# Multi-query attention on one core: the next batch's query loads and DMA transposes dealt out over the whole batch

## The chip, the cores and the metric

The kernel runs on one core of a Trainium2 chip. The metric is the device time of one execution in microseconds (us). Three runs of the kernel before gave 773.25, 774.67 and 776.23 us; the median is 774.67 us.

## The reference

Softmax attention with 16 query heads that share one key head and one value head. There are 8 batches of 1024 positions, and a head has 64 elements. All tensors are float32.

```
scores = np.matmul(q, k.transpose(0, 1, 3, 2)) / np.sqrt(head_dim)
weights = np.exp(scores - np.max(scores, axis=-1, keepdims=True))
weights = weights / np.sum(weights, axis=-1, keepdims=True)
attn_out = np.matmul(weights, v)
```

## The kernel before, in words

**Steps.** The work is cut into 1024 steps, 128 for each batch: eight pairs of heads, for each pair two chunks of 512 queries, for each chunk eight blocks of 128 keys. `step(u)` makes the scores of one block for two heads: two TensorE matmuls (L249) fill one PSUM tile `sc` of 128 x 1024 float32. There are three `sc` buffers. Four of five steps take the exponential on ScalarE (ACTIVATE, L262, 824 of them). Each fifth step takes it on VectorE by arithmetic on the bits (`vector_exp`: L213 reads the PSUM tile and frees it; L219, L229, L237 and L239 follow, SBUF to SBUF). The program recorded which buffer each `sc` tile gets: after a VectorE step the buffer comes back three steps later, and in some places four.

**Values.** The product with V runs some 18 steps behind the scores, as many small matmuls (L323) into PSUM tiles `ot` of seven groups, of which there are two. When a tile is full, VectorE inverts the sums (L265) and scales the result (L274), and SyncE stores it (L302). After the last group of a batch VectorE also tests the range of the sums (function `check`: L369, L375 and L379 over 128 columns); this falls at steps 21 to 27 of the next batch.

**The order of the work.** The order is written out by hand: each engine and each DMA queue takes its instructions in the order in which Python emits them, and waits on semaphores. `plan()` deals the value matmuls over the steps, and `after(u)`, called behind step u, emits the preparation of the next batch b+1:

- `load_kv` (L99, on SyncE): K of the next batch into `knat`.
- `load_v` (L106, on GpSimd): V into one of two constant tiles `vp`; it must wait until TensorE has used the V that lies there, which is that of batch b-1.
- `load_q` (L123, on GpSimd): 128 rows of queries, cast to fp16, into one of eight `q16` buffers. Eight of these in a batch.
- `turn_q` (L133, on SyncE): a DMA transpose of one such buffer into the tile `qt`, of which there are two. Eight in a batch.
- `prep_k` (L192, on GpSimd): two TENSOR_SCALAR that scale K into fp16, followed on SyncE by one DMA transpose (L196) into `k2t`.
- `prep_v` (L204, on VectorE): two small TENSOR_SCALAR that scale V.

Before, these stand at steps 48 (K and V), 48 to 62 (a query load in every second step), 64 to 78 (a transpose in every second step), 84 (`prep_k`) and 88 (`prep_v`) of the batch. The scores of the next batch read the first half of `qt` from step 128 and the second half from step 136 (counted from the start of batch b).

GpSimd's queue has nothing else in it. So GpSimd does not run at the steps at which its work is emitted: it runs ahead until an instruction has to wait. SyncE's queue also has the 129 stores, each of which waits for its L274; this holds SyncE near the step at which its work was emitted.

Of the kernel before, what the change touches and what calls it, by code (L numbers as in the profile page):

```python
# [30 lines left out]
def attention_main(ctx, tc, q, k, v, out, flag):  # L31
# [14 lines left out]
    NKT = S // P  # L46
# [46 lines left out]
    def load_kv(b):  # L93
        st = kv.setdefault(b, {})
        st["knat"] = kvp.tile([P, NKT, D], FP32, tag="knat", name=f"knat{b}")
        n = 2 if b == 0 else 1
        for h in range(n):
            js = slice(h * NKT // n, (h + 1) * NKT // n)
            nc.sync.dma_start(  # L99
                out=st["knat"][:, js, :],  # L100
                in_=k[b].rearrange("(c p) d -> p c d", p=P)[:, js, :],
            )
        st["vp"] = vps[b % 2]

    def load_v(b):
        nc.gpsimd.dma_start(  # L106
            out=vps[b % 2][:, 0, :, 0:D], in_=v[b].rearrange("(c p) d -> p c d", p=P)
        )
# [10 lines left out]
    def load_q(b, c):  # L119
        h0 = 2 * NFIRST if b == 0 else 0  # L120
        t = q16p.tile([P, H * D], FP16, tag="q16", name=f"q16_{b}_{c}")
        q16[(b, c)] = t[:, h0 * D :]
        nc.gpsimd.dma_start(  # L123
            out=q16[(b, c)],
            in_=q[b, c * P : (c + 1) * P, h0:, :].rearrange("p h d -> p (h d)"),
        )

    def turn_q(b, c):

        p0 = NFIRST if b == 0 else 0  # L130
        if b not in qt:
            qt[b] = qtp.tile([P, HP, S], FP16, tag="qt", name=f"qt{b}")
        nc.sync.dma_start_transpose(  # L133
            out=qt[b][:, p0:, c * P : (c + 1) * P], in_=q16.pop((b, c))
        )

    def bank(name):
        return op.tile([P, 512], FP32, tag="ot", name=name)
# [32 lines left out]
    def first_q(ps, p, cs):  # L171
        for c in cs:
            nc.tensor.matmul(  # L173
                ps[:, c * P : (c + 1) * P],
                q16[("first", p)][:, c, :],
                ident16,
                is_transpose=True,
                start=True,
                stop=True,
            )  # L180

    def first_q_out(ps, p, cs, eng):
        if 0 not in qt:
            qt[0] = qtp.tile([P, HP, S], FP16, tag="qt", name="qt0")
        at = slice(cs[0] * P, (cs[-1] + 1) * P)
        eng(out=qt[0][:, p, at], in_=ps[:, at])  # L186

    def prep_k(b):
        st = kv[b]
        k16d = kvp.tile([P, NKT, 2, D], FP16, tag="k16d", name=f"k16d_{b}")  # L190
        for i in range(2):
            nc.gpsimd.tensor_scalar(  # L192
                out=k16d[:, :, i, :], in0=st["knat"], scalar1=kscale, scalar2=None, op0=ALU.mult
            )
        st["k2t"] = kvp.tile([P, S], FP16, tag="k2t", name=f"k2t{b}")
        nc.sync.dma_start_transpose(  # L196
            out=st["k2t"].rearrange("p (j s) -> p j s", j=NKT),
            in_=k16d.rearrange("p j i d -> p (j i d)"),
        )

    def prep_v(b):
        vp = kv[b]["vp"]
        for i, ci in ((1, C0), (2, C3)):
            nc.vector.tensor_scalar(  # L204
                out=vp[:, i, :, 0:D], in0=vp[:, 0, :, 0:D], scalar1=ci, scalar2=None, op0=ALU.mult
            )
# [176 lines left out]
    PSTEPS = NCH * NKT  # L383
# [38 lines left out]
    def after(u):  # L422
        p, r = divmod(u, PSTEPS)
        b, hp = divmod(p, HP)
        if u == 1:
            first_q(turned[0], 0, range(NKT // 2, NKT))
            first_q_out(turned[0], 0, range(NKT // 2, NKT), nc.vector.tensor_copy)
        if r == 7 and p + 1 < NFIRST:
            turned[p + 1] = bank(f"qps{p + 1}").bitcast(FP16)
            first_q(turned[p + 1], p + 1, range(NKT))  # L430
            first_q_out(turned[p + 1], p + 1, range(NKT), nc.vector.tensor_copy)
        if b + 1 < B:
            at = hp * PSTEPS + r - 3 * PSTEPS
            if at == 0:
                load_kv(b + 1)
                load_v(b + 1)
            if 0 <= at < 2 * NKT and at % 2 == 0:
                load_q(b + 1, at // 2)
            at -= PSTEPS
            if 0 <= at < 2 * NKT and at % 2 == 0:  # L440
                turn_q(b + 1, at // 2)
            at -= PSTEPS
            if at == 4:
                prep_k(b + 1)
            if at == 8:
                prep_v(b + 1)

    with tc.manual_schedule():
        load_kv(0)
# [31 lines left out]
        for u in range(STEPS):  # L481
# [27 lines left out]
            for x in us:  # L509
                after(x)  # L510
# [97 lines left out]
@with_exitstack  # L608
def kernel(ctx, tc, q, k, v, out):
    nc = tc.nc  # L610
    fp = ctx.enter_context(tc.tile_pool(name="flagp", bufs=1))
    flag = fp.tile([1, 1], I32, name="flag")
    attention_main(tc, q, k, v, out, flag)
    bad = nc.values_load(flag, min_val=0, max_val=1)
    with tc.If(bad != 0):
        attention_general(tc, q, k, v, out)
# [30 lines left out]
```

## Time and profile before

| what | value |
|---|---|
| median of three runs | 774.67 us (773.25 to 776.23) |
| the profiled execution | 773.22 us |
| its span, first to last instruction | 771.4 us |
| granted TensorE clock, mean | 0.998 |
| GpSimd busy | 66.9 us (9%) |
| DMA engines: share of queue 1 (SyncE's) and queue 0 (GpSimd's) | 32.7% and 15.2% |
| mean rate of all DMA | 96 GB/s |
| stores of 256 KB, issue to landing, median | 2.5 us |
| query loads of 256 KB, issue to landing, median | 8.7 us |

A group's row in the page gives its line, engine and operation, what it writes and reads, the count, the busy time, the mean duration in ns, and the idle time of the engine just before it with what ended it. ScalarE's instructions overlap: one ACTIVATE is recorded with 1085 ns, but the next starts about 904 ns behind it (the median of the 823 intervals between their starts in the trace). [...] "SPq" is SyncE's queue.

### The profile page before, as it was taken

The page shows a single profiled execution, that of the slowest core. Times are in us where ns is not written, and L with a number is a line of the kernel's source. Part 1 is how long each engine was busy: PE and PEld are TensorE (multiplying, and loading weights), DVE is VectorE, ACT ScalarE, POOL GpSimd, SP SyncE. Part 2 cuts the span into 40 slices and gives each one's busy share as a digit, 9 for nine tenths or more (in the row PEclk, how much of TensorE's full clock was granted, in tenths as well). Part 3 has the DMA queues.
Part 4 walks back from the last instruction along what each step waited for, and adds up shares of the span by engine and source line. Part 5 has one row for each costly group of instructions (what it writes and reads, how often), then busy time and mean ns, then how long its engine had stood idle before and what let it go on. Part 6 is the DMA issues. An engine that isn't in the chain of part 4 may idle for free.

```text
span 771.4 us, 30670 instructions
## 1 busy us (share of the span) xinstructions
PE 744.1 (96%) x13474; PEld 471.9 (61%) x13474; DVE 730.3 (95%) x1349; ACT 759.3 (98%) x827; POOL 66.9 (9%) x99
## 2 busy tenths in 40 slices
PE   6999999999999999999999999999999999999997
PEld 2566666666666666666666666666666666666665
DVE  3899999999999999999999999999999999999993
ACT  7999999999999999999999999999999999999996
POOL 4110002100111002010020100200002100000000
PEclk9999999999999999999999999999999999999999
DMA  9949219471283814657246552566516474111112
GB/s 176 149 88 166 57 43 159 91 146 57 38 165 85 150 30 79 137 112 110 57 88 141 114 97 57 82 134 117 106 43 121 96 137 85 43 44 56 44 44 85
DMA packets 168633, 73.84 MB, mean 96 GB/s; under 512 B 93744, under 2 KB 161328, under 8 KB 168496
## 3 DMA queue, kind: packets, MB, share of 16 engines
q1 hardware_dynamic: 148864, 53.76, 32.7%
q0 software_dynamic: 18576, 17.57, 15.2%
q8 instruction: 106, 1.74, 1.0%
q10 hardware_dynamic: 1056, 0.52, 0.3%
q14 instruction: 31, 0.25, 0.1%
HBM read 37.75 MB, written 33.55 MB: 92 GB/s over the span
## 4 chain that ended last, share of the span: by engine, by line
PE 40%; ACT 35%; issue 12%; DVE 12%; DMA 1%; ACTq 0%; DVEq 0%
ACT wt L262 35%; PE ot L323 22%; PE sc L249 18%; DVE we L213 4%; DVE osb L274 2%; DVE we L239 2%; DVE mm L237 2%; DVE we L229 1%; DVE m L219 1%; DMA qf<-in_q_dram 1%; DVE rec_all L265 0%; PE otl L353 0%; DVE both L375 0%; DVE ok_all L379 0%; DVE ge L369 0%
## 5 line engine op out<-in xcount | busy, mean ns | idle before, releaser
L262 ACT ACTIVATE wt<-sc 128x1024 f16<-128x1024 f32 x824 | 756.8, 1085 | 2.0 <-PE sc L249 1.7
L323 PE MATMUL ot<-vp,wt 128*128 128x65 f16 x6528 | 430.1, 194 | 0.8 <-DVE osb L274 0.8
L323 PEld LDWEIGHTS <-wt 128*128 128x128 f16 x6528 | 328.2, 98 | 133.7 <-issue 133.5
L249 PE MATMUL sc<-qt,k2t 64*128 64x512 f16 x2048 | 364.6, 388 | 16.2 <-ACT wt L262 12.1
L323 PE MATMUL ot<-vp,we 128*128 128x65 f16 x4800 | 351.7, 193 | 0.0
L323 PEld LDWEIGHTS <-we 128*128 128x128 f16 x4800 | 251.6, 97 | 44.4 <-issue 44.4
L213 DVE TENSOR_SCALAR we<-sc 128x1024 int16<-128x1024 f32 x200 | 243.4, 1217 | 12.0 <-PE sc L249 11.1
L249 PEld LDWEIGHTS <-k2t 64*128 64x128 f16 x2048 | 86.3, 94 | 108.7 <-issue 75.7
L237 DVE TENSOR_TENSOR mm<-m 128x1024 f16<-128x1024 f16 x200 | 136.4, 682 | 0.0
L239 DVE TENSOR_TENSOR we<-we,mm 128x1024 f16<-128x1024 f16 x200 | 136.1, 681 | 0.0
L274 DVE TENSOR_TENSOR osb<-ot,rec_all 128x448 f32<-128x448 f32 x146 | 90.7, 621 | 5.1 <-DVE rec_all L265 0.2
L219 DVE TENSOR_SCALAR m<-we 128x1024 int16<-128x1024 int16 x200 | 85.8, 429 | 0.0
L229 DVE TENSOR_SCALAR we<-we 128x1024 int16<-128x1024 int16 x200 | 85.3, 426 | 0.0
L106 POOL DMA_DIRECT2D vp<-in_v_dram x8 | 7.8, 980 | 377.7 <-PE ot L323 377.6
L123 POOL DMA_DIRECT2D q<-in_q_dram x64 | 34.5, 570 | 26.3 <-DMA qt<-q 22.5
L265 DVE RECIPROCAL rec_all<-ot 128x7 f32<-128x7 f32 x146 | 28.5, 195 | 7.2 <-PE ot L323 7.2
L192 POOL TENSOR_SCALAR k16d<-knat 128x512 f16<-128x512 f32 x14 | 22.4, 1611 | 137.7 <-DMA knat<-in_k_dram 115.9
L157 PE MATMUL kps<-ident,k 128*64 128x128 f16 x16 | 1.3, 314 | 4.4 <-DVE k L148 4.4
L204 DVE TENSOR_SCALAR vp<-vp 128x512 f16<-128x512 f16 x16 | 3.9, 284 | 1.5 <-DMA vp<-in_v_dram 1.5
L186 DVE COPY qt<-qps 128x512 f16<-128x512 f16 (+1 forms) x2 | 1.1, 554 | 4.0 <-PE qps L173 4.0
L157 PEld LDWEIGHTS <-k 128*64 128x64 f16 x16 | 0.8, 159 | 4.6 <-DVE k L148 4.6
L466 ACT ACT_TABLE_LOAD x1 | 1.3, 1283 | 1.9 <-issue 1.9
(29 smaller groups left out, 22.4 us busy)
## 6 DMA issues: line engine op xcount, KB each, us to landing
out_dram<-osb SPq DMA_DIRECT2D x127, 256.0 KB, 2.5
q<-in_q_dram POOLq DMA_DIRECT2D x56, 256.0 KB, 8.7
knat<-in_k_dram SPq DMA_DIRECT2D x7, 256.0 KB, 3.7
q<-in_q_dram POOLq DMA_DIRECT2D x8, 192.0 KB, 7.4
vp<-in_v_dram POOLq DMA_DIRECT2D x8, 128.0 KB, 4.1
qt<-q SPq DMA_TRANSPOSE x64, 3.7
qf<-in_q_dram ACTq DMA_DIRECT2D x2, 256.0 KB, 4.3
knat<-in_k_dram SPq DMA_DIRECT2D x2, 128.0 KB, 3.6
```

The lines of the kernel that those rows point to most:

```text
L123: nc.gpsimd.dma_start(out=q16[(b, c)], in_=q[b, c * P : (c + 1) * P, h0:, :].rearrange("p h d -> p (h d)"),)
L192: nc.gpsimd.tensor_scalar(out=k16d[:, :, i, :], in0=st["knat"], scalar1=kscale, scalar2=None, op0=ALU.mult)
L213: nc.vector.tensor_scalar(out=t, in0=sc, scalar1=15.0 * 1024, scalar2=0.0, op0=ALU.add, op1=ALU.max)
L219: lambda: nc.vector.tensor_scalar(out=m.bitcast(I16), in0=t, scalar1=0x3FF, scalar2=0x3C00, op0=ALU.bitwise_and, op1=ALU.bitwise_or,)
L229: lambda: nc.vector.tensor_scalar(out=w3[:, 0].bitcast(I16), in0=t, scalar1=0x7C00, scalar2=None, op0=ALU.bitwise_and,)
L237: pend.append(lambda: nc.vector.tensor_tensor(out=m2, in0=m, in1=m, op=ALU.mult))
L239: lambda: nc.vector.tensor_tensor(out=w3[:, 2], in0=w3[:, 1], in1=m2, op=ALU.mult)
L249: nc.tensor.matmul(sc[:, hh, :], k2t[r : r + 64, j * P : (j + 1) * P], qt[b][r : r + 64, p % HP, c * QCH : (c + 1) * QCH], start=True, sto ...
L262: nc.scalar.activation(out=w, in_=sc, func=EXP, scale=escale, bias=math.log(CS))
L265: nc.vector.reciprocal(out=rec_all[:, g0 : g0 + n], in_=o[:, 0:n, D])
L274: nc.vector.tensor_tensor(out=ob[:, i0 : i0 + n, :], in0=o[:, 0:n, 0:D], in1=rec.unsqueeze(2).broadcast_to([P, n, D]), op=ALU.mult,)
L323: nc.tensor.matmul(o[:, gg % GB, 0 : D + 1], w[:, hh, qb * P : (qb + 1) * P], vp[:, i, j, 0 : D + 1], start=(n == 0), stop=last,)
```

## The change

Only the places in `after(u)` change, no instruction. K's load moves from step 48 to step 2, V's from 48 to 30, `prep_k` from 84 to 58 and `prep_v` from 88 to 72. The eight query loads move to steps 4, 17, 30, ... 95 and the eight transposes to steps 24, 37, 50, ... 115, both 13 steps apart.

```
         if b + 1 < B:
-            at = hp * PSTEPS + r - 3 * PSTEPS
-            if at == 0:
+            at = hp * PSTEPS + r
+            if at == 2:
                 load_kv(b + 1)
+            if at == 30:
                 load_v(b + 1)
-            if 0 <= at < 2 * NKT and at % 2 == 0:
-                load_q(b + 1, at // 2)
-            at -= PSTEPS
-            if 0 <= at < 2 * NKT and at % 2 == 0:
-                turn_q(b + 1, at // 2)
-            at -= PSTEPS
-            if at == 4:
+            if at == 58:
                 prep_k(b + 1)
-            if at == 8:
+            if at == 72:
                 prep_v(b + 1)
+            c, late_by = divmod(at - 4, 13)
+            if 0 <= c < NKT and late_by == 0:
+                load_q(b + 1, c)
+            c, late_by = divmod(at - 24, 13)
+            if 0 <= c < NKT and late_by == 0:
+                turn_q(b + 1, c)
```

The order of the built program shows what this does on each engine. TensorE's and ScalarE's instructions stand as before, and so do the reuse of the `sc` buffers and all waits between the compute engines. On VectorE `prep_v` stands some 20 instructions earlier in each batch. On SyncE the transposes stand one by one between the stores. On GpSimd the order within a batch was V, eight query loads, `prep_k`; it is now query loads 0 and 1, V, query loads 2, 3 and 4, `prep_k`, query loads 5, 6 and 7.

## Prediction
> **What bounds the kernel now.** I read the page's busy times first, then ScalarE's group, then the waits around the places where ScalarE loses time.
>
> ```profile
> PE 744.1 (96%) x13474; PEld 471.9 (61%) x13474; DVE 730.3 (95%) x1349; ACT 759.3 (98%) x827; POOL 66.9 (9%) x99
> ...
> L262 ACT ACTIVATE wt<-sc 128x1024 f16<-128x1024 f32 x824 | 756.8, 1085 | 2.0 <-PE sc L249 1.7
> ```
>
> ScalarE is idle for only 2.0 us ahead of its 824 ACTIVATEs. In the trace the first starts at 7.2 us and the last ends at 765.4 us, and most intervals between starts are 0.903 to 0.904 us. The floor of that stretch is 823 x 0.9033 + 1.1 = 744.5 us; it takes 758.1 us, so 13.6 us are above the floor. I added up this excess by sixteenths of a batch (columns of 16 steps, over all eight batches): steps 64 to 79, with nearly all query transposes, have 1.35 us; steps 96 to 111, which have no preparation at all, have 1.33 us. The columns of steps 16 to 31 and 32 to 47 have 3.11 and 2.20 us. So **the transposes cost ScalarE nothing today, and spreading them has nothing to win**. The excess behind step 16 has one other source:
>
> ```profile
> 497.92 0.22 DVE L369 TENSOR_SCALAR ge<-rec_all 128x128 f32<-128x128 f32 x1
> 498.17 0.29 DVE L375 SCALAR_TENSOR_TENSOR both<-rec_all,ge 128x128 f32<-128x128 f32 x1
> 498.50 0.29 DVE L379 TENSOR_REDUCE ok_all<-both 128x1 f32<-128x128 f32 x1
> 498.70 1.21 DVE L213 TENSOR_SCALAR we<-sc 128x1024 int16<-128x1024 f32 x1
> ```
> ```profile
> PE sc L249 <- DVE we L213: 0.4, 1, 0.4
> ACT wt L262 <- PE sc L249: 0.4, 1, 0.4
> ```
>
> This is VectorE's timeline in batch 5, and the waits of 495 to 501 us. The range test takes 0.78 us (497.92 to 498.70). L213 starts late by that much, the `sc` buffer comes back late, TensorE waits for it, and ScalarE for TensorE. VectorE cannot absorb it: a cycle of five steps lasts 3.00 us without a result tile (L213 at 498.70, the next at 501.70) and 3.77 us with one (314.69 to 318.46), and five of seven cycles have one: 3.55 us on average, against 4 x 0.903 = 3.61 us of ScalarE. That is **0.06 us of slack per five steps**. Taking 0.29 us as a batch's usual excess over steps 16 to 47, the range tests cost 0, 0.35, 0.52, 0, 0.60, 0.56 and 0.26 us in batches 1 to 7, together 2.3 us. (In batch 0 the 0.7 us at 20 to 24 us come ahead of the full TensorE clock; the edit does not touch them.)
>
> A stall begins where L213 starts more than some 0.92 us behind the preceding ACTIVATE if its buffer returns after three steps (L213's 1.17 us and the two matmuls with ScalarE's start, 0.62 us, against 3 x 0.903 us), or 1.82 us after four. Behind the range test that distance is 1.32, 1.69, 1.12, 1.37, 1.49 and 1.43 us in batches 1 to 6; in 1, 2, 4 and 6 the buffer at that place returns after four. So any VectorE delay that meets the range test is paid nearly in full by ScalarE, there or within 25 steps (the distance still reaches 0.98 at step 48 of batch 4).
>
> **What the change moves.** GpSimd is not where its steps say. V's load waits for TensorE, and all behind it follows at once:
>
> ```profile
> 115.25 0.95 POOL L106 DMA_DIRECT2D vp<-in_v_dram  x1 [62.08 <-PE ot L323]
> 116.20 4.29 POOL L123 DMA_DIRECT2D q<-in_q_dram  x8
> ```
> ```profile
> L192 POOL TENSOR_SCALAR k16d<-knat 128x512 f16<-128x512 f32 x14 | 22.4, 1611 | 137.7 <-DMA knat<-in_k_dram 115.9
> ```
>
> First GpSimd's timeline in batch 1, at step 16: V and eight query loads in one go, although emitted at steps 48 to 62. Below it the page's row of `prep_k`: its wait is for K, which SyncE loads at step 48, so it runs at steps 43 to 58, far from the range test.
>
> *Query loads.* They do not spread as written. Loads 0 and 1 now stand ahead of V, in the batch before, behind their `q16` buffers' transposes. Loads 2 to 7 still follow V's wait. No transposition needs them before step 50. Price nothing.
>
> *K and `prep_k`.* K is loaded at step 2 and lands some 3.7 us (5 steps) after its issue, ahead of step 16. So `prep_k` no longer waits for K: it follows V (0.95 us) and three query loads (3 x 0.53 us), 2.54 us behind V's start, for 2 x 1.48 us. That is steps 19 to 24, **just ahead of the range test**. What it does to VectorE is seen in batch 2 (timelines of VectorE and of GpSimd):
>
> ```profile
> 234.79 0.42 DVE L219 TENSOR_SCALAR m<-we 128x1024 int16<-128x1024 int16 x1
> 235.13 0.83 DVE L229 TENSOR_SCALAR we<-we 128x1024 int16<-128x1024 int16 x1
> ```
> ```profile
> 235.07 2.95 POOL L192 TENSOR_SCALAR k16d<-knat 128x512 f16<-128x512 f32 x2 [20.60 <-DMA knat<-in_k_dram]
> ```
>
> L229 starts 0.06 us into the GpSimd instruction and takes 0.83 instead of 0.42 us. Over the seven executions of `prep_k`, L219 and L229 together were lengthened by 0.41, 0.58, 0.41, 0.41, 0.41, 0.27 and 0.61 us; the other VectorE instructions were not. Putting the new place (V's start + 2.54 us) on the old timeline: in batches 1, 2, 4 and 5 an L219 starts inside it (117.82, 212.70, 400.93 and 495.71 us); in 3 and 6 none does, by 0.4 us and less. I take one hit of 0.41 us in each of the four (1.64), and half a hit in each of the two (0.41). The query loads that stand there now already lengthen L219 and L229 by 0.19, 0.04 and 0.17 us in batches 2, 4 and 5; this goes with the loads that are displaced: -0.40. `prep_k` in its old place costs ScalarE about 0.1 us (batch 6, steps 48 to 63, 0.27 against 0.19): -0.1. Both ends: no hit at all, -0.5; two hits in all six batches, 12 x 0.41 = +4.9. I take the rows' own places, nearer the lower end. Batch 0's `prep_k` comes at some 31 us, with no range test near: nothing.
>
> [...]
>
> *Transposes.* Same 64, dispatched in 1.3 us each on SyncE.
>
> ```profile
> qt<-q SPq DMA_TRANSPOSE x64, 3.7
> ```
>
> The last one is emitted at step 115 and needed when TensorE, some two steps ahead, scores step 136: 19 steps x 0.73 us = 14 us against 3.7 us to landing. The fourth stands at step 63 and is needed at 126. Stores that queue behind one transpose wait 1.3 us; an output buffer is reused a whole tile (seven stores, about 40 us) later, so nobody waits. If a transpose took the trace's maximum of 14.8 us (at the start, beside eight loads), that cover would be gone.
>
> *`prep_v`.* Two instructions of 0.28 us go from step 88 to 72. At 88 no excess is seen (1.45 us in that column against 1.33); at 72 the distance is 0.3 to 0.8 us and will be less without `prep_k` shortly before. V has landed long since. Price nothing.
>
> **Sum:** 1.64 + 0.41 - 0.40 - 0.1 = +1.5 us on the profiled 773.22 us (span 771.4 and 1.8 around it): 774.8. The median shown is 1.45 us above that execution, so I add the same to it: **776.2 us**, +0.2%. About 0.5% (3.9 us) is what a measurement here can tell from no change.
>
> **Rivals.**
>
> 1. *No hit counts* (0.20): the GpSimd instructions fall between L229 and the next L219, or the delay falls into VectorE's waits (0.04 us from TensorE's end before batch 3's step 21). -0.5 us: 774.2. For it: batches 3 and 6 do this on the old timeline. Against: all seven old executions hit.
> 2. *Clearly slower: the result banks* (0.16). A later VectorE also empties `ot` later, and TensorE with 96% busy has to wait for a bank, as in batch 6 (waits of 596 to 601 us):
>
> ```profile
> PE ot L323 <- DVE osb L274: 0.5, 1, 0.5
> ```
>
> It decides once L274 behind the range test ends later than TensorE's first matmul of the next-but-one tile, as there. Six full hits (2.5) and five more such waits of 0.5 us: +5.0, 779.7 us. Against: only 0.8 us of such waits in the whole span.
> [...]
> 4. *A late transpose* (0.02): at 14.8 us to landing, TensorE waits about 1 us at seven batch ends: +8.5 with the sum above, 783.
> 5. *Faster by over 0.5%* (0.02): all 2.3 us of range test stalls and more would have to go; no row shows how.
>
> My forecast has 0.56. Range 773.2 to 779.8 us: from rival 1 less 1 us of run-to-run spread to the upper bound of the hits, which takes in rival 2. Faster by over 0.5% 0.03, within 0.5% 0.77 (forecast, rival 1, most of rival 3), slower 0.20 (rivals 2, 4, and the forecast's upper tail).
>
> **What would show it.** In the profile after: L192 right behind three L123 at steps 19 to 24 with no wait for K in batches 1 to 6; L219 or L229 of 0.8 us there; more excess at steps 24 to 48 in batches 1, 2, 4, 5; transposes with no TensorE wait behind them. If L192 still runs at steps 43 to 58, or the excess behind the range test does not grow, I am wrong. If TensorE waits at steps 128 or 136, rival 4 holds.

## The result, and the profile after

The changed kernel takes 783.53 us (median of 6 runs, 782.05 to 786.79), the kernel before 773.97 us on the same chip (6 runs, 773.25 to 776.23): **slower by 1.2%, ratio 1.0123 (95% interval 1.0104 to 1.0141)**. The forecast was +0.2%, 776.2 us, with a range up to 779.8. The profiled execution of the changed kernel took 782.26 us, its span is 780.4 us and its mean granted clock 0.992.

First the page of the kernel after: busy times, three groups (busy, mean ns of one, idle time before them and what ended it) and one row of DMA issues. The last line here is L219's group in the kernel before.

```profile
PE 743.4 (95%) x13474; PEld 472.1 (60%) x13474; DVE 736.0 (94%) x1349; ACT 760.6 (97%) x827; POOL 67.4 (9%) x99
...
L262 ACT ACTIVATE wt<-sc 128x1024 f16<-128x1024 f32 x824 | 758.1, 1082 | 9.7 <-PE sc L249 9.0
...
L219 DVE TENSOR_SCALAR m<-we 128x1024 int16<-128x1024 int16 x200 | 89.0, 445 | 0.0
...
L192 POOL TENSOR_SCALAR k16d<-knat 128x512 f16<-128x512 f32 x14 | 22.9, 1648 | 12.3 <-DMA knat<-in_k_dram 12.3
...
qt<-q SPq DMA_TRANSPOSE x64, 4.0
```
```profile
L219 DVE TENSOR_SCALAR m<-we 128x1024 int16<-128x1024 int16 x200 | 85.8, 429 | 0.0
```

ScalarE now waits 9.7 us ahead of its ACTIVATEs, where it waited 2.0. VectorE is busy for 736.0 us instead of 730.3 with the same 1349 instructions, so some of them became longer: L219 from 429 to 445 ns on average. L192's wait for K fell from 115.9 to 12.3 us, all of it in batch 0. The transposes land 4.0 us after their issue (median; before 3.7).

The waits over the whole span (total us, times, longest) show the way on which the time reaches ScalarE, first after, then before:

```profile
ACT wt L262 <- PE sc L249: 9.0, 12, 1.5
PE sc L249 <- DVE we L213: 7.4, 8, 1.6
...
PE ot L323 <- DVE osb L274: 1.8, 4, 0.7
```
```profile
ACT wt L262 <- PE sc L249: 1.7, 4, 0.7
...
PE sc L249 <- DVE we L213: 1.0, 3, 0.4
...
PE ot L323 <- DVE osb L274: 0.8, 2, 0.5
```

TensorE waits 7.4 us for L213 (before: 1.0 us), and for a result bank it waits 1.8 us (before: 0.8). It has no wait for a transpose in this profile.

The excess over ScalarE's floor of 0.9033 us per ACTIVATE, added up as in the prediction, went from 13.58 to 22.53 us: +8.95, which is nearly the whole difference of the two profiled executions (782.26 - 773.22 = 9.04). By sixteenths of a batch it was 1.32, 3.11, 2.20, 1.46, 1.35, 1.45, 1.33, 1.36 us; it is 1.34, **10.19, 4.41**, 1.14, 1.37, 1.41, 1.34, 1.34. So all of the increase lies at steps 16 to 47, in batches 1 to 6. The columns in which the transposes used to stand alone (64 to 79) did not move.

GpSimd's and VectorE's timelines at that place in batch 1:

```profile
115.03 0.91 POOL L106 DMA_DIRECT2D vp<-in_v_dram  x1 [71.31 <-PE ot L323]
115.92 1.62 POOL L123 DMA_DIRECT2D q<-in_q_dram  x3
117.53 3.64 POOL L192 TENSOR_SCALAR k16d<-knat 128x512 f16<-128x512 f32 x2
```
```profile
117.01 0.75 DVE L239 TENSOR_TENSOR we<-we,mm 128x1024 f16<-128x1024 f16 x1
117.68 2.14 DVE L219 TENSOR_SCALAR m<-we 128x1024 int16<-128x1024 int16 x1
119.75 0.82 DVE L229 TENSOR_SCALAR we<-we 128x1024 int16<-128x1024 int16 x1
```

`prep_k` follows V and three query loads, 2.50 us behind V's start (forecast 2.54), at step 19. But the L219 that meets it takes 2.14 us instead of 0.42, and L229 0.82. The forecast had one lengthening of 0.41 us here. Batch 4, the same two engines:

```profile
406.60 3.65 POOL L192 TENSOR_SCALAR k16d<-knat 128x512 f16<-128x512 f32 x2
```
```profile
406.99 1.04 DVE L219 TENSOR_SCALAR m<-we 128x1024 int16<-128x1024 int16 x1
407.95 0.95 DVE L229 TENSOR_SCALAR we<-we 128x1024 int16<-128x1024 int16 x1
408.83 1.08 DVE L237 TENSOR_TENSOR mm<-m 128x1024 f16<-128x1024 f16 x1
```

Three VectorE instructions in a row are lengthened, by 0.62, 0.54 and 0.40 us (undisturbed they take 0.42, 0.42 and 0.68). L237 was never lengthened in the profile before. I call the sum over a batch, of what each VectorE instruction beside GpSimd takes above its undisturbed time, the **lengthening**. In batches 1 to 6 it is 2.20, 2.05, 0.42, 1.67, 0.96 and 1.35 us: 8.64 us in all, mean 1.44 (of the 8.64, L219 has 5.0, L229 1.9, L237 1.2 and L239 0.5). In the kernel before it was 0.44 to 0.74, mean 0.54.

And batch 2, where the delay meets the range test:

```profile
214.76 2.15 DVE L219 TENSOR_SCALAR m<-we 128x1024 int16<-128x1024 int16 x1
...
218.67 0.22 DVE L369 TENSOR_SCALAR ge<-rec_all 128x128 f32<-128x128 f32 x1
...
219.45 1.22 DVE L213 TENSOR_SCALAR we<-sc 128x1024 int16<-128x1024 f32 x1
```

L213 starts 3.54 us behind the preceding ACTIVATE; by the prediction's estimate the stall begins at 0.92 or 1.82. Behind the range test the largest distance before was 1.69 us.

### The profile page after: what moved, and what is told of

The parts are those of the page before. It is cut to its first block, busy times and chain, and to the rows that moved or that the text cites. A ratio compares the mean times of both kernels' runs of the same rounds, so it can differ in the third digit from the quotient of the medians.

```text
span 780.4 us, 30655 instructions
## 1 busy us (share of the span) xinstructions
PE 743.4 (95%) x13474; PEld 472.1 (60%) x13474; DVE 736.0 (94%) x1349; ACT 760.6 (97%) x827; POOL 67.4 (9%) x99
## 4 chain that ended last, share of the span: by engine, by line
PE 38%; ACT 34%; DVE 14%; issue 12%; DMA 1%; DVEq 0%; ACTq 0%
ACT wt L262 34%; PE ot L323 21%; PE sc L249 17%; DVE we L213 4%; DVE mm L237 2%; DVE osb L274 2%; DVE we L239 2%; DVE m L219 2%; DVE we L229 1%; DMA qf<-in_q_dram 1%; DVE rec_all L265 0%; DMA out_dram<-osb 0%; PE otl L353 0%; DVE both L375 0%; DVE ok_all L379 0%
## 5 line engine op out<-in xcount | busy, mean ns | idle before, releaser
L262 ACT ACTIVATE wt<-sc 128x1024 f16<-128x1024 f32 x824 | 758.1, 1082 | 9.7 <-PE sc L249 9.0
L213 DVE TENSOR_SCALAR we<-sc 128x1024 int16<-128x1024 f32 x200 | 243.5, 1217 | 15.9 <-PE sc L249 15.3
L237 DVE TENSOR_TENSOR mm<-m 128x1024 f16<-128x1024 f16 x200 | 137.7, 688 | 0.0
L239 DVE TENSOR_TENSOR we<-we,mm 128x1024 f16<-128x1024 f16 x200 | 136.8, 684 | 0.0
L219 DVE TENSOR_SCALAR m<-we 128x1024 int16<-128x1024 int16 x200 | 89.0, 445 | 0.0
L229 DVE TENSOR_SCALAR we<-we 128x1024 int16<-128x1024 int16 x200 | 85.6, 428 | 0.0
L192 POOL TENSOR_SCALAR k16d<-knat 128x512 f16<-128x512 f32 x14 | 22.9, 1648 | 12.3 <-DMA knat<-in_k_dram 12.3
```

Source lines behind the costliest of these rows:

```text
L192: nc.gpsimd.tensor_scalar(out=k16d[:, :, i, :], in0=st["knat"], scalar1=kscale, scalar2=None, op0=ALU.mult)
L213: nc.vector.tensor_scalar(out=t, in0=sc, scalar1=15.0 * 1024, scalar2=0.0, op0=ALU.add, op1=ALU.max)
L219: lambda: nc.vector.tensor_scalar(out=m.bitcast(I16), in0=t, scalar1=0x3FF, scalar2=0x3C00, op0=ALU.bitwise_and, op1=ALU.bitwise_or,)
L229: lambda: nc.vector.tensor_scalar(out=w3[:, 0].bitcast(I16), in0=t, scalar1=0x7C00, scalar2=None, op0=ALU.bitwise_and,)
L237: pend.append(lambda: nc.vector.tensor_tensor(out=m2, in0=m, in1=m, op=ALU.mult))
L239: lambda: nc.vector.tensor_tensor(out=w3[:, 2], in0=w3[:, 1], in1=m2, op=ALU.mult)
```

## The experiments

Each ratio is against the kernel before on the same chip, with its 95% interval. "Lengthening" is per batch, mean of batches 1 to 6, from the run's profile.

**1. Only K goes back** (`e1_k_late`). K's load returns to step 48; the rest of the change stays.

```
-            if at == 2:
+            if at == 48:
                 load_kv(b + 1)
```

> The changed kernel with one edit undone: K is loaded at step 48 again, so that prep_k waits for it and runs at steps 43 to 58 as before; query loads 5, 6 and 7 stay behind it. All transposes and loads stay spread. Theory A (the whole loss is prep_k running on GpSimd between the query loads, just ahead of the range test): the time falls back to that of the kernel before, 773 to 775 us, and the excess of steps 16 to 47 from 14.6 to about 5.3 us. Rival B (the spread transposes, stores behind them, or the two early query loads cost): it stays at 780 us or more. If 6 of the 9.6 us go, both have a part.

775.5 us (773.3 to 777.97), ratio 1.0020 (1.0003 to 1.0037), just above what was expected; lengthening 0.47. With K late, `prep_k` waits for it again and starts at steps 45 to 60. 7.8 of the 9.6 us are gone (+1.8 left), with all the transposes and loads in their new places. In the profile of this run the rest has a place of its own: steps 32 to 47 of batch 0, where TensorE waits for one of batch 0's query transposes.

```profile
PE sc L249 <- DMA qt<-q: 2.0, 1, 2.0
```

The first transpose of batch 1 now stands close behind those of batch 0, and took 9.1 us to dispatch. But experiment 10, whose transposes stand as in the kernel before, has the same wait with 0.9 us, so that the change causes it is not shown.

**2. Only `prep_k` moves** (`e2_k_early_alone`). The kernel before, with K's load at step 2 and `prep_k` behind the third query load; loads and transposes stay as they were.

```
+            if hp == 0 and r == 2:
+                load_kv(b + 1)
             if at == 0:
-                load_kv(b + 1)
                 load_v(b + 1)
...
+            if at == 4:
+                prep_k(b + 1)
```

> The kernel before with prep_k moved alone: K is loaded at step 2, and prep_k stands behind V and three query loads on GpSimd, as in the changed kernel; the transposes stay in their burst at steps 64 to 78. Theory A: 781 to 785 us, with L219 and L229 lengthened by some 1.4 us a batch at steps 19 to 24. Rival B: 774 to 776 us.

780.05 us (779.28 to 781.64), ratio 1.0082 (1.0057 to 1.0106), just under what was expected; lengthening 1.31. So the move of `prep_k` alone makes 0.8 of the 1.2%. In this profile the granted clock does not fall (0.998 on average) and TensorE has no wait for nothing that the profile shows; the changed kernel's profile has both (see the last section). What makes the other 0.4% was not separated; a repeat of the changed kernel (9) gave 0.9%.

**3. No `prep_k`** (`e11_no_prep_k`). The changed kernel; batches 2 to 7 take the keys of batch 1, without `prep_k` and its transpose, so their scores are of the wrong keys.

```
+        if b > 1:
+            st["k2t"] = kv[1]["k2t"]
+            return
```

> The changed kernel with prep_k left out for batches 2 to 7: they use the transposed K of batch 1, so the scores of these batches are of the wrong keys; K is still loaded. Loads, transposes and stores stay as in the changed kernel. Theory A: with no TENSOR_SCALAR on GpSimd in batches 1 to 6, the time is that of the kernel before or a little less, 772 to 774.5 us; what is above 773 is the price of the spread transposes beside the burst of loads. Rival B: 777 us or more.

773.83 us (772.57 to 776.58), ratio 0.9997 (0.9981 to 1.0013). With the 64 transposes and 64 loads in their new places, nothing is lost. Together the three say: the loss needs `prep_k` on GpSimd at its new place, and without it the new places of loads and transposes cost nothing measurable here.

**4. No range test** (`e3_no_range_test`). My theory in the prediction was that a small delay costs because it meets the range test. Here the test of batches 0 to 6 is left out and their result set to 1.

```
+        if g1 < NG - GRP:
+            return
```

> The changed kernel without the range test of batches 0 to 6 (L369, L375 and L379 are left out there, and their result is set to 1), so 0.8 us less on VectorE at steps 21 to 27. Theory A, with the meeting of prep_k and range test as what makes the loss: VectorE is lengthened as before by some 1.4 us a batch, but ScalarE starts to stall only past a distance of 0.92 us (1.82 where the buffer returns after four steps), so some 0.6 to 0.9 us a batch stay: 774 to 777 us. If the lengthening alone makes the loss and the range test does not matter: 780 us or more, less only the 2.3 us that the range tests cost before.

780.98 us (778.07 to 782.93), ratio 1.0085 (1.0061 to 1.0110): the reading by which only the meeting matters is missed by 4 us. Its waits over the span:

```profile
ACT wt L262 <- PE sc L249: 9.0, 8, 1.6
PE sc L249 <- DVE we L213: 4.5, 7, 1.6
...
PE ot L323 <- issue: 4.3, 3, 1.5
```

TensorE still waits up to 1.6 us for L213 with no range test ahead of it: the lengthening alone (2.20, 2.05, 0.74, 1.67, 0.96, 1.38 us) carries L213 past the distance. Steps 16 to 47 of batches 1 to 6 are 7.3 us above their usual excess, with the range test 11.6. So the test adds to the loss, but it isn't the condition. It adds more than it cost by itself: in batches 1 and 4, where it cost nothing in the kernel before, the excess is 0.5 us lower without it. The median alone says less: 2.9 us of this profile's excess lie in batch 0, in stretches that the changed kernel's profile does not have, and the last line shows 4.3 us in which TensorE waited for nothing that the profile shows (see the last section).

**5. `prep_k` ahead of V** (`e4_k_before_v`). In the changed kernel `prep_k` is emitted at step 29, ahead of V's load at 30. It then no longer follows V's wait, and runs at steps 5 to 15 (in batch 5 at 2 to 6).

```
+            if at == 29:
+                prep_k(b + 1)
             if at == 30:
                 load_v(b + 1)
-            if at == 58:
-                prep_k(b + 1)
```

> The changed kernel with prep_k emitted just ahead of V's load: on GpSimd it then runs when K has landed, at steps 8 to 14, with no query load next to it and some ten steps ahead of the range test. [...] Reading A2 (prep_k lengthens VectorE by up to 1.7 us wherever it meets it in an unlucky place): 1 us a batch and more, 777 to 781 us.

774.25 us (773.08 to 775.36), ratio 0.9999 (0.9988 to 1.0010), below the 777 to 781 us of reading A2; lengthening 0.55, with 1.07 in batch 2. The loss is gone with one instruction pair moved by some ten steps.

**6. Is it the query loads beside it?** (`e5_loads_inside`) As 5, but with query loads 2 to 4 between the two halves of `prep_k`. GpSimd's own issuing of the loads might be what turns 0.4 us into 1.4.

```
             if i == 1:
                 for c in (2, 3, 4):
                     load_q(b, c)
```

> As the run with K ahead of V (prep_k at steps 8 to 14), but query loads 2, 3 and 4 are emitted between the two GpSimd instructions of prep_k: the first has no query load ahead of it, the second has three right ahead. Reading A1 (the loads ahead of prep_k make the lock on VectorE long): where VectorE's L219, L229, L237 or L239 meet the second instruction, they are lengthened by more than 0.41 us, up to 1.7, and the sum is 0.8 to 1.7 us a batch; the first alone does 0.41 or less. Reading A2 (only the place against VectorE's cycle counts): both instructions lengthen alike, 0.2 to 0.6 us a batch in all. Time 774 to 779 us by A1, 774 to 776 us by A2.

776.39 us (776.0 to 776.83), ratio 1.0031 (1.0010 to 1.0051). Lengthening 0.89, 1.35, 1.35, 0.89, 1.20, 0.45 us, mean 1.02, twice that of 5, but in parts of at most 0.54 us. It lies between the two theories.

**7. No query load anywhere near** (`e6_loads_ahead`). Each query load is emitted one batch earlier, behind the transpose that frees its buffer, so that loads really stand 13 steps apart; `prep_k` follows V directly, with no load around it.

```
-            if at == 30:
+            if at == 22:
                 load_v(b + 1)
-            if at == 58:
+            if at == 23:
                 prep_k(b + 1)
...
                 turn_q(b + 1, c)
+                if b + 2 < B:
+                    load_q(b + 2, c)
```

> The changed kernel with each query load emitted behind the transpose that frees its buffer, one batch earlier: so the loads really run one by one on GpSimd, 13 steps apart, and none stands next to prep_k, which stays behind V at steps 17 to 22, just ahead of the range test. Reading A1: VectorE is lengthened by 0.4 to 0.6 us a batch, time 775 to 777.5 us. Reading A2: 1.0 to 1.5 us a batch as in the changed kernel, time 779 to 784 us.

778.47 us (778.32 to 778.97), ratio 1.0062 (1.0045 to 1.0078). Lengthening 0.46, 0.31, 2.38, 0.41, 0.64 and 1.94 us, mean 1.02 (and 2.05 in batch 0). GpSimd and VectorE in batch 3:

```profile
305.43 0.90 POOL L106 DMA_DIRECT2D vp<-in_v_dram  x1 [16.26 <-PE ot L323]
306.35 3.77 POOL L192 TENSOR_SCALAR k16d<-knat 128x512 f16<-128x512 f32 x2
```
```profile
305.78 0.93 DVE L239 TENSOR_TENSOR we<-we,mm 128x1024 f16<-128x1024 f16 x1
306.64 2.14 DVE L219 TENSOR_SCALAR m<-we 128x1024 int16<-128x1024 int16 x1
```

Again an L219 of 2.14 us, and no query load in sight. The theory that the loads beside `prep_k` are needed falls; the price lies in the meeting of L192 with VectorE at this place. That it lies between the changed kernel and the kernel before was in neither expectation. The mean lengthening equals that of 6, but here it comes in lumps of about 2 us (batches 0, 3 and 6), and the time is 2 us longer (778.47 against 776.39). The profile of 7 has 2.5 us more excess than that of 6, of which 1.5 us stand in batch 0, whose lump the mean leaves out. Two explanations of the rest remain and were not separated: lumps go past what L213's distance still allows, or the place nearer to the range test costs more.

**8. The same with `prep_k` ahead of V** (`e7_loads_ahead_k_first`). As 7, with V's load and `prep_k` exchanged (the edit is shown against the changed kernel).

```
-            if at == 30:
+            if at == 22:
+                prep_k(b + 1)
+            if at == 23:
                 load_v(b + 1)
-            if at == 58:
-                prep_k(b + 1)
```

> As the run with the loads a batch ahead, and prep_k ahead of V too, at steps 5 to 14: no query load and no range test near it, and no burst of loads behind V either. Theory A: what GpSimd costs ScalarE is gone but for 0.3 to 0.5 us a batch of VectorE time in a quiet place: 772.5 to 775 us, the kernel before or slightly faster, the excess of steps 16 to 47 at 5 us or less. If spread transposes and stores cost by themselves: 776 us and more, with long dispatches of transposes and TensorE waiting for nothing that the profile shows.

773.64 us (773.21 to 774.41), ratio 0.9996 (0.9984 to 1.0008). Batch 1:

```profile
109.14 0.68 DVE L239 TENSOR_TENSOR we<-we,mm 128x1024 f16<-128x1024 f16 x1
109.74 0.67 DVE L219 TENSOR_SCALAR m<-we 128x1024 int16<-128x1024 int16 x1
110.33 0.41 DVE L229 TENSOR_SCALAR we<-we 128x1024 int16<-128x1024 int16 x1
```

One L219 lengthened by 0.25 us, and each batch has one such hit by `prep_k` of 0.25 to 0.42 us. In this kernel loads and transposes are both truly dealt out over the batch, and it is as fast as the kernel before, to within some 0.1%: **dealing them out wins nothing and costs nothing that could be measured here**.

**9. The change once more** (`e9_after_again`). The changed kernel unaltered, for a second profile.

> The changed kernel once more, for a second profile of it. Theory A says that the lengthening of VectorE behind V is the same in kind: 1.0 to 1.7 us a batch on average in batches 1 to 6. What the first profile shows once each should not come back at the same place: the stretch at half the granted clock in batch 2, and TensorE's wait for nothing at step 43 of batch 3. If both come back there, they belong to the change and not to the single execution. Time 782 to 787 us.

781.25 us (781.14 and 781.37, two runs), ratio 1.0087 (1.0055 to 1.0119), a little under what was expected. Lengthening 2.20, 1.14, 0.41, 1.66, 0.96, 1.35 us: five batches repeat within 0.01 us, batch 2 has 1.14 instead of 2.05. So in five of six batches the lengthening follows from the order of the work; what decided it in batch 2 is not shown. The stretch at half the granted clock did not come back, TensorE's wait for nothing at step 43 of batch 3 did (1.4 us).

**10. The range test taken apart** (`e8_test_split`). The kernel before, with the three instructions of the range test 15, 30 and 45 steps later than they stood. It tries the prediction's reading of what bounds the kernel. (The added lines put `vector_exp` and all behind it two lines lower in this kernel and the next: L215 for L213, L264 for L262.)

```
+        for i, f in enumerate(parts):
+            if g1 < NG - GRP:
+                later[now[0] + 15 * (i + 1)] = f
+            else:
+                f()
...
+        now[0] = u
+        if u in later:
+            later.pop(u)()
```

> The kernel before with one edit: the three instructions of the range test stand 15, 30 and 45 steps behind their old place instead of back to back. It tests the distance rule that the prediction used: each then adds 0.2 to 0.3 us to VectorE's distance instead of 0.78 at once, and stays under 0.92 us in most places. By the rule the 2.3 us of stalls behind the range test fall to under 1 us: 772 to 773.3 us, against 773.7 of the kernel before. If VectorE's total work and not the distance at one place sets the time, no change: 773.5 to 774.5 us.

772.47 us (771.61 to 773.78), ratio 0.9987 (0.9977 to 0.9997). The excess over steps 16 to 47 falls to 0.27, 0.38, 0.39, 0.27, 0.40, 0.27 and 0.39 us in batches 1 to 7: nearly all of the 2.3 us that the prediction put down to the range test are gone. The median gains 1.0 us. Not all of the rest is accounted for: the profiled execution (773.78 us) is the slowest of its ten, with 1.65 us more excess in batch 0 (TensorE waits 0.9 us for a query transpose and 0.8 us for nothing that the profile shows) and 0.8 us more at steps 48 to 63, where parts of the test now stand.

**11. Both together** (`e10_quiet`). 8 with 10.

> The loads a batch ahead, K ahead of V, and the range test split, in one kernel: all that the runs so far point to. By theory A and the distance rule nothing on GpSimd meets a late VectorE any more: 770.5 to 772.5 us, below the kernel before (773.5) and below the split test alone (772.47). If the spread transposes cost something of their own that the burst of loads hid: 772.5 to 774 us.

772.2 us (771.79 to 772.74) against 773.99, ratio 0.9974 (0.9964 to 0.9985): the fastest of all, 0.26% below the kernel before. Its page:

```profile
L264 ACT ACTIVATE wt<-sc 128x1024 f16<-128x1024 f32 x824 | 756.2, 1085 | 1.1 <-PE sc L251 1.0
```

ScalarE's idle time falls from 2.0 to 1.1 us. The split test alone (10) gave half of this gain, and 8 alone gave none that is clear of noise; whether the other half is chance, or the two help each other, is open.

## Why the prediction was wrong

**Right.** *What bounds the kernel:* ScalarE's floor, 0.06 us of VectorE slack per five steps, and the distance of L213. Experiment 10 removes nearly all the stalls that this accounts for. *Nothing to win from the transposes:* 3, 5 and 8 are at 0.9997, 0.9999 and 0.9996. *The query loads do not spread:* three follow V at once (115.92 us above). *`prep_k` moves to steps 19 to 24 in batches 1 to 6, with no wait for K:* 2.50 us behind V's start. *It lengthens VectorE, and ScalarE pays nearly in full:* in batches 1, 4 and 5 the excess grew by 2.2, 1.6 and 0.8 us, which is what VectorE's lengthening there grew by; in batch 6 it grew by 0.6, about half of that. *No late transpose:* no wait at steps 128 or 136 (the waits for a transpose that some runs show, up to 2.0 us in experiment 1, are all in batch 0 and for its own queries). *The old place:* its column fell by 0.3 us (forecast 0.1).

**Wrong: the price of a meeting.** The step that failed is "I take one hit of 0.41 us in each of the four (1.64), and half a hit in each of the two (0.41)". This term, +2.05, measured 8.64 us of lengthening. Batches 1, 2, 4 and 5 were hit as named (2.20, 2.05, 1.67, 0.96), but 3 and 6 as well (0.42, 1.35), and not once each: two to three instructions in a row, L237 and L239 among them, and in batches 1 and 2 an L219 by 1.73 us. The upper bound, "12 x 0.41 = +4.9", was not a bound. It took the largest single lengthening of seven executions, all of which had met VectorE at another place, for the most that a meeting can cost.

**Wrong: that a hit ends after 0.41 us.** The row of batch 2 of the kernel before (L229 starts 0.06 us into an L192 and takes 0.83 instead of 0.42 us) shows that VectorE can get through inside a GpSimd instruction, not that it always does. Both happen here. In batch 1 L219 starts 0.16 us into the first L192 and does not get through before that has ended (1.58 us long); it ends 0.71 us later. In batch 4 L219 starts 0.39 us into the first L192 (1.89 us long) and ends 0.46 us before it does, after 1.04 us. The four L219 that the prediction named were lengthened by 1.73, 1.73, 0.62 and 0.27 us. In four batches of experiment 8 an L219 or L229 that starts 0.07 to 0.59 us into one gets through after 0.41 us more, and in three of these it is L192 that becomes longer (1.92 to 2.22 us instead of 1.5). What in the chip sets these times is not shown.

The prediction had left L237 and L239 out, since none was lengthened before: in the kernel before, twelve L237 and L239 started inside an L192 and took 0.67 to 0.70 us. In batch 4 of the changed kernel an L237 that started inside an L192 took 1.08 instead of 0.68 us.

**Wrong in part: the range test as the condition.** Experiment 4 shows that it adds to the stall; a lengthening of 1.4 to 2.2 us passes the distance by itself.

**The size.** With 8.64 in place of 2.05 the prediction's sum gives 783 us, against 783.53. That is closer than it deserves. In the profile after, two things that no rival had add about 2 us (last section), and slack absorbs nearly as much; that the two cancel is luck. The second profile of the same kernel, with 0.9 us less lengthening in batch 2 and without the fall of the clock, was 1 us shorter.

**Open.** What decides between +0.27, +0.41 and +1.73 us. In all nine cases of about +1.73 us (four kernels and the repeat) the L239 just ahead of the L219 had itself been lengthened, by 0.07 to 0.31 us, by an L192 or by GpSimd's issuing of a load; in no case was it undisturbed. But fifteen other L239, lengthened by 0.06 us and more, were followed by an L219 of +0.26 to +0.41 only. In batch 2 of the changed kernel L192 starts 0.34 us into L239 in both profiles; the sums are 2.05 and 1.14 us. So start times to 0.01 us did not tell which it would be, and no experiment here tried it alone.

## What to carry to other kernels

A GpSimd instruction that lengthened VectorE had no fixed price here: when it was moved beside other VectorE work, what its old neighbours paid was no upper bound. One VectorE instruction paid 0.41 us at most at the old place and up to 1.73 us at others, which is more than a whole L192 takes by itself (1.5 us). On GpSimd's queue, which runs ahead, the place of an instruction was set by the wait ahead of it: one loosened wait (K's load, 46 steps earlier; 115.9 us of waiting fell to 12.3) moved `prep_k` by some 30 steps to just ahead of the range test, while emitting it ahead of V's wait made the same edit free (ratio 0.9999). Where a second engine has only 0.06 us of slack per cycle against the one that bounds the kernel, short work on it is worth taking apart (1.0 us in 10, 1.8 us in 11). Dealing out transfers that nobody waits for won nothing (ratio 0.9996 in 8).

## What the runs showed of the hardware that I had not expected

**The clock fell after a stall that was no full stop.** Windows of the profile after, in batch 2 (length, busy time and count of PE, PEld, DVE, ACT and POOL, then granted clock, DMA share and GB/s):

```profile
218.10:221.50 3.40, 1.42 (x25) 0.82 (x23) 3.30 (x7) 2.08 (x3) 0.10 (x1) 1.00 1.13 212
221.50:225.00 3.50, 3.50 (x45) 2.04 (x42) 3.47 (x7) 1.98 (x3) 0.00 (x0) 0.51 1.27 209
```

In the first 3.4 us TensorE is busy for 1.42 us, between waits of 0.67 us for a bank and 1.31 us for L213. Then it is granted half its clock (0.51 in this window) for 3.4 us, and two more ACTIVATEs come 0.79 and 0.73 us late. Experiment 9 at the same place:

```profile
219.00:222.40 3.40, 2.15 (x39) 1.21 (x37) 3.38 (x7) 2.63 (x4) 0.13 (x1) 1.00 1.11 207
222.40:225.90 3.50, 3.50 (x69) 2.20 (x66) 3.46 (x7) 3.48 (x4) 0.00 (x0) 1.00 1.18 212
```

TensorE is busy for 2.15 of 3.4 us, and the clock stays at 1.00. In the changed kernel's clock record the fall lasts 3.41 us, and TensorE had been busy for 42% of the 3.41 us ahead of it. I divided all 13 profiles into stretches of that length that end where the clock changed. From 25 us on, the clock fell after stretches of up to 42% and stayed after those of 49% and more; before that it also fell after some of 38 to 59%. So the busy share alone does not decide. Here the fall goes with 1.5 us more of waiting on ScalarE; no run tried it by itself.

**TensorE waited for nothing that the profile shows, perhaps because of a slow transpose.** Of the 56 dispatches of a query transpose for batches 1 to 7 on SyncE, 16 took over 1.8 us in the profile after (up to 6.5), against 6 before (up to 2.2): the five longest, at steps 25 to 32, now stand where the burst of query loads is on its way. In batch 3, 11 steps behind one of 5.84 us, TensorE is idle for 0.82 us:

```profile
329.19 0.20 PE L323 MATMUL ot<-vp,wt 128*128 128x65 f16 x1 [0.82 <-issue]
```

"issue" says that it waited for nothing that the profile shows. A packet of instructions (16 KB) began to arrive 1.2 us ahead of step 43's ACTIVATE, where it came 3.7 us ahead of that step in the kernel before. The same gap was 1.4 us in experiment 9 and 1.5 us in experiment 4, whose transposes there took 6.5 and 7.7 us to dispatch and whose packets came 0.6 us ahead. It was absent in 3 and 5, with dispatches of 2.7 and 1.3 us there, and in 2, which has no transpose there; their packets came 3.3 to 4.4 us ahead. Two more gaps stand in batch 0 of experiment 4 (1.3 and 1.5 us) and one in batch 0 of experiment 10 (0.8 us), whose transposes stand as before. Against it, dispatches of 3.8 to 6.5 us in batches 2, 5 and 6 of the changed kernel had no gap behind them. That the transpose delays the packet, or that TensorE waited for this packet, is not shown.
